# Ten seven-product weight pairs in place of eight, with their weight sums on GpSimd

## The chip, the cores and the metric

The kernel runs on one core of a Trainium2 chip (trn2). The metric is the device time of one execution in microseconds (us). The time before is 927.12 us, the median of 3 runs (926.98 to 927.13).

## What is computed

One decoder layer over 512 tokens with 1024 channels, all in fp32: an RG-LRU branch and a sparse-attention branch, merged by gates, then a feed-forward part (ConvGLU) and a gated per-layer embedding. The change lies in the up projection of the feed-forward part:

```python
xn = _rmsnorm(x, ffn_norm[l])
up = xn @ w_up[l]                     # (512, 1024) @ (1024, 6144)
g_ffn = _causal_dwconv(up[..., :D_FF], ffn_conv_w[l], ffn_conv_b[l])
x = x + (jax.nn.gelu(g_ffn) * up[..., D_FF:]) @ w_down[l]
```

## The kernel before, in words

**Layout.** Channels lie on the 128 partitions and the 512 tokens along the free dimension. Weights are tiles of 128 x 1024 numbers (8 blocks of 128 x 128, one for each 128 input channels). Every fp32 operand of a product is split into a high and a low part in the format fp32r: a cast on ScalarE (ACT) makes the high part, a subtraction on VectorE (DVE) the low one (`split`, L92 to L97; `pair`, L114). One product block is then three matmuls (`three`, L99 to L102): high x high, high x low, low x high. So an output tile of 128 x 512 is 8 x 3 = 24 matmuls of 512 columns on TensorE (PE).

**Order of the work.** The list `order` holds one entry per weight tile or pair of tiles; the main loop (L1013) runs its entries in turn. `feed` (L998) splits weights some entries ahead and issues the next loads on SyncE's (SP) queue. `whi` and `wlo` have four buffers each, `raw` two. What the program text gives is a priority: outside the start (a hand-written schedule), the instructions of each engine are put in order by a scheduler at build time, which lets an instruction go ahead of its place when its inputs and buffers are free in its reckoning. On the chip each engine then takes its instructions in that fixed order.

**The feed-forward part** takes the 24 channel blocks f of the hidden layer in three groups of eight. In each group the up projection comes first: per f the gate half (`up_g`, L586) and the value half (`up_u`, L606), 48 matmuls of 512 columns, which I call an ordinary pair. The gate half passes a three-tap convolution and a GELU (`up_act`, L596), and is multiplied by the value half (L610). In the first group the factor `rstd` of the norm is applied to the products, once on DVE (L591) and once on GpSimd (L603), since it isn't ready earlier; the later groups work on an input that already has it. Then eight down-projection steps (`dn_step`, L613) add the group's part to the residual `F`.

**Seven-product pairs.** For some f of the second and third group (`SEVEN`, L45: 8, 10, ..., 22) gate and value half are done together as a 2 x 2 block product over (first 512 and last 512 input channels) x (gate and value) with half the tokens each, in Strassen's manner: seven products instead of eight, each 4 blocks x 3 matmuls of 256 columns, 84 matmuls in all. They need four weight operands (a, b, c, d), each with a high and a low part, and sums of the input (`xsum`, made by `seven_x`, L168, ahead of the second group). For a pair i:

- `seven_load` (L133) loads both weight tiles into `pairraw` (one buffer, 2 x 512 KB, two transfers on SP's queue).
- `seven_first` (L146) splits the gate tile (operand a, into `whi` and `wlo`) and makes the sums `pairsum` (L153, L154).
- `seven_second` (L156) splits these sums into operand b and makes two more sums in place in `pairraw` (L159, L160).
- `seven_third` (L162) splits the result into c, `seven_last` (L165) splits half of the value tile into d.
- `seven_step` (L189) runs the products, collects them in the PSUM banks p1 to p4 (`aux`, five banks) and drains them on DVE (L218, L220, L224, L229, L233 to L235).

The tiles `bhi`, `blo`, `chi`, `clo`, `dhi`, `dlo`, `pairraw` and `pairsum` have one buffer each. The products stand in the text as a, a, b x sx(0), c x sx(1), c x gx(4), b x sx(2), d; between the last two writes into p3 the text has a read of p3:

```python
prod(p3[:, :h], c, 512, gx(4, second))                            # L223
nc.vector.tensor_add(gp[:, 2 + h:], gp[:, 2 + h:], p3[:, :h])     # L224
...
prod(p3[:, h:], b, 0, sx(2))                                      # L228
```

Of the kernel before, what the change touches and what calls it, by code (L numbers as in the profile page):

```python
# [41 lines left out]

SEG = [0, 128, 384, 768]

SEVEN = tuple(range(8, 24, 2))  # L45
PTO = [0, 512, 1024, 896]


# [1 line left out]
def layer(ctx: ExitStack, tc: tile.TileContext, xT, pT, wall, vwi, vec, relb, onehot, out):  # L50
# [25 lines left out]
    def aux_tile():  # L76
        return psum.tile([128, T], F32, name="aux", bufs=5)
# [53 lines left out]
        return i < len(order) and order[i][0] is None  # L131

    def seven_load(i):  # L133
        f = SW["of"][i]
        SW[i] = r = P["pool"].tile([128, 2, WCOL], F32, name="pairraw")
        for z in range(2):
            nc.sync.dma_start(r[:, z], wall[S_UP + 2 * f + z])

    def seven_pair(i, name, src):
        n = src.shape[1]  # L140
# [5 lines left out]
    def seven_first(i):  # L146
        r = SW[i]
        HI[i] = base.tile([128, WCOL], F32R, name="whi", bufs=NSPL)
        LO[i] = base.tile([128, WCOL], F32R, name="wlo", bufs=NSPL)
        nc.scalar.copy(HI[i], r[:, 0])  # L150
        nc.vector.tensor_sub(LO[i], r[:, 0], HI[i].bitcast(F32))
        s = SW[i, "s"] = P["pool"].tile([128, WCOL], F32, name="pairsum")
        nc.vector.tensor_add(s[:, :512], r[:, 0, :512], r[:, 1, :512])  # L153
        nc.vector.tensor_add(s[:, 512:], r[:, 1, :512], r[:, 1, 512:])  # L154

    def seven_second(i):  # L156
        r, s = SW[i], SW[i, "s"]
        seven_pair(i, "b", s)
        nc.vector.tensor_add(r[:, 0, :512], s[:, 512:], r[:, 0, :512])  # L159
        nc.vector.tensor_add(r[:, 0, 512:], r[:, 0, :512], r[:, 0, 512:])  # L160

    def seven_third(i):  # L162
        seven_pair(i, "c", SW[i][:, 0])

    def seven_last(i):  # L165
        seven_pair(i, "d", SW[i][:, 1, 512:])

    def seven_x(j):  # L168

# [16 lines left out]
        nc.vector.scalar_tensor_tensor(d, b, -1.0, y[1][:, :h], op0=OP.mult, op1=OP.subtract)  # L186
        pair(SW["x"][:, j], t)

    def seven_step(i, f):  # L189
        h = T // 2  # L190
        XG, X = P["XG"], SW["x"]
        first, second = slice(0, h), slice(h, T)

        def prod(o, w, at, x):
            for j in range(4):
                s = slice(at + j * 128, at + (j + 1) * 128)
                xh, xl = x(j)
                three(o, w[0][:, s], w[1][:, s], xh, xl, j == 0, j == 3)

        def gx(k0, t):  # L200
            return lambda j: (XG[:, k0 + j, 0, t], XG[:, k0 + j, 1, t])

        def sx(z):
            t = slice(z * h, (z + 1) * h)
            return lambda j: (X[:, j, 0, t], X[:, j, 1, t])

        seven_third(i)
        a, b, c = (HI[i], LO[i]), SW[i, "b"], SW[i, "c"]
        keep = tmp()
        p1, p2 = aux_tile(), aux_tile()  # L210
        prod(p1[:, :h], a, 0, gx(0, first))
        nc.scalar.copy(keep[:, :h], p1[:, :h])
        seven_last(i)
        prod(p2[:, :h], a, 512, gx(4, first))
        feed(i + 1)
        prod(p2[:, h:], b, 512, sx(0))
        prod(p1[:, h:], c, 0, sx(1))
        nc.vector.tensor_add(keep[:, h:], keep[:, :h], p1[:, h:])  # L218
        gp = P["gp"][f % 2]
        nc.vector.tensor_add(gp[:, 2:], keep, p2)  # L220
        feed(i + 2)
        p3 = aux_tile()
        prod(p3[:, :h], c, 512, gx(4, second))  # L223
        nc.vector.tensor_add(gp[:, 2 + h:], gp[:, 2 + h:], p3[:, :h])  # L224
        if seven(i + 3):
            feed(i + 3)
        g = up_act(f, gp)
        prod(p3[:, h:], b, 0, sx(2))  # L228
        nc.vector.tensor_add(keep[:, h:], keep[:, h:], p3[:, h:])  # L229
        p4 = aux_tile()  # L230
        prod(p4[:, :h], SW[i, "d"], 0, sx(3))
        t = tmp()
        nc.vector.tensor_add(t[:, h:], keep[:, h:], p2[:, h:])  # L233
        nc.vector.tensor_add(t[:, :h], keep[:, h:], p4[:, :h])
        nc.vector.scalar_tensor_tensor(t, t, -1.0, g, op0=OP.mult, op1=OP.mult)  # L235
        defer(pair, hp(f), t)


    urgent, patient, later = [], [], []
# [13 lines left out]
    def defer(f, *a):  # L253
        later.append((f, a))
# [599 lines left out]
    for m in range(8):  # L854
        add(S_OUT + m, lambda i, m=m: out_step(i, m), 0.0,
            open_ffn if m == 0 else (lambda m=m: load_x(m + 1) if m + 1 < 8 else None))
    SW["of"] = {}
    for g in range(3):
        for f in range(8 * g, 8 * g + 8):
            if f in SEVEN:  # L860
                SW["of"][len(order)] = f
                order.append((None, lambda i, f=f: seven_step(i, f), 0.0, None))
                continue
            add(S_UP + 2 * f, lambda i, f=f: up_g(i, f, [(7, stats)] if f == 0 else []))
            add(S_UP + 2 * f + 1, lambda i, f=f: up_u(i, f))
# [129 lines left out]
    n = len(order)  # L995
    at = [9, 11]

    def feed(upto):  # L998
        while at[0] <= min(upto, n - 1):
            i = at[0]  # L1000
            if seven(i):
                seven_first(i)
            else:
                split(i)
            at[0] += 1
            while at[1] < min(at[0] + 2, n):
                if seven(at[1]):
                    seven_load(at[1])
                else:
                    load(at[1])  # L1010
                at[1] += 1

    for i in range(8, n):  # L1013
        if not seven(i):
            feed(i + (1 if seven(i + 1) else 2))
        run_deferred()
        if seven(i + 1):
            seven_second(i + 1)
        _, fn, budget, before = order[i]
        if before:  # L1020
# [68 lines left out]
```

## Time and profile before

| | |
|---|---|
| Median of 3 runs | 927.12 us (926.98 to 927.13) |
| The profiled execution | 926.65 us |
| Its span in the profile | 924.9 us |
| PE busy | 913.7 us (99%), 4486 matmuls |
| DVE busy | 660.7 us (71%) |
| ACT busy | 457.6 us (49%) |
| GpSimd (POOL) busy | 16.1 us (2%) |
| Moved by DMA | 97.24 MB, mean 105 GB/s |

The span is the time from the first to the last recorded instruction. Busy time of PE is modelled, since matmuls overlap: the distance between the starts of neighbouring matmuls tells more of its pace than their durations. PEld is the load of weights into PE, which runs beside the matmuls. A wait is put down to whatever ended last before the waiting instruction started.

### The profile page before, as it was taken

What the parts mean: (1) busy time and instruction counts of PE and PEld (TensorE: products, weight loads), DVE (VectorE), ACT (ScalarE), POOL (GpSimd) and SP (SyncE); (2) the same over time, 40 slices, a digit from 0 to 9 for tenths busy, and PEclk for the clock granted to TensorE, in tenths of its full rate; (3) what the DMA queues carried; (4) which work ended last, traced back from release to release, by engine and by line L of the source; (5) the groups of instructions that cost most, each with busy time, mean ns of one, the idle gap of its engine ahead of it and who ended that gap; (6) DMA issues with size and microseconds to landing.
All of it is one profiled execution on the core that took longest, in us unless ns stands there. A gap on an engine that the chain in (4) does not pass through costs nothing.

```text
span 924.9 us, 11724 instructions
## 1 busy us (share of the span) xinstructions
PE 913.7 (99%) x4486; PEld 770.9 (83%) x4486; DVE 660.7 (71%) x1081; ACT 457.6 (49%) x662; POOL 16.1 (2%) x25
## 2 busy tenths in 40 slices
PE   7999999999999999999999999999999999999998
PEld 6988778888888788888888888888888899988886
DVE  6589798899975877655567557987863587655653
ACT  7477849953223677632444335635542254434530
POOL 0001000000000000000001110000000000000000
PEclk9999999999999999999999999999999999999999
DMA  7463123224233221224532332233322322222231
GB/s 265 121 212 131 46 92 112 70 92 137 92 114 125 80 68 47 69 91 150 176 108 92 98 107 91 69 114 114 114 90 93 115 91 91 91 90 93 91 114 45
DMA packets 31447, 97.24 MB, mean 105 GB/s; under 512 B 3736, under 2 KB 4760, under 8 KB 31392
## 3 DMA queue, kind: packets, MB, share of 16 engines
q1 hardware_dynamic: 31088, 96.38, 31.8%
q8 instruction: 35, 0.57, 0.3%
q10 hardware_dynamic: 304, 0.12, 0.1%
q14 instruction: 20, 0.16, 0.1%
HBM read 92.27 MB, written 4.74 MB: 105 GB/s over the span
## 4 chain that ended last, share of the span: by engine, by line
PE 62%; ACT 2%; DVE 0%; issue 0%; ACTq 0%
PE acc L100 17%; PE acc L101 17%; PE acc L102 17%; PE aux L100 4%; PE aux L101 4%; PE aux L102 4%; ACT E L503 0%; ACT L768 0%; PE aux L516 0%; ACT whi L96 0%; DVE PT L118 0%; ACT L503 0%; ACT gb L768 0%; ACT PT L117 0%; ACT gb L534 0%; DVE tmp L656 0%
## 5 line engine op out<-in xcount | busy, mean ns | idle before, releaser
L96 ACT CAST whi<-raw 128x1024 fp32r<-128x1024 f32 (+1 forms) x140 | 146.1, 1046 | 225.1 <-PE acc L101 165.5
L100 PE MATMUL acc<-XN,whi 128*128 128x512 f32 x632 | 248.8, 394 | 5.0 <-ACT whi L685 5.0
L101 PE MATMUL acc<-XN,whi 128*128 128x512 f32 x632 | 247.9, 392 | 0.0
L102 PE MATMUL acc<-XN,wlo 128*128 128x512 f32 x632 | 247.5, 392 | 0.0
L97 DVE TENSOR_TENSOR wlo<-raw,whi 128x1024 fp32r<-128x1024 f32 (+1 forms) x140 | 169.6, 1214 | 36.7 <-ACT whi L96 36.0
L100 PEld LDWEIGHTS acc<-XN,whi 128*128 128x128 f32 x632 | 119.3, 189 | 28.7 <-ACT whi L685 5.0
L102 PEld LDWEIGHTS acc<-XN,wlo 128*128 128x128 f32 x632 | 119.2, 189 | 24.9
L101 PEld LDWEIGHTS acc<-XN,whi 128*128 128x128 f32 x632 | 119.3, 189 | 24.2 <-DVE XN L121 0.7
L100 PE MATMUL acc<-XG,whi 128*128 128x512 f32 x320 | 124.6, 389 | 0.0
L101 PE MATMUL acc<-XG,whi 128*128 128x512 f32 x320 | 124.6, 389 | 0.0
L102 PE MATMUL acc<-XG,wlo 128*128 128x512 f32 x320 | 124.5, 389 | 0.0
L102 PEld LDWEIGHTS acc<-XG,wlo 128*128 128x128 f32 x320 | 60.1, 188 | 12.6
L100 PEld LDWEIGHTS acc<-XG,whi 128*128 128x128 f32 x320 | 60.1, 188 | 12.2
L101 PEld LDWEIGHTS acc<-XG,whi 128*128 128x128 f32 x320 | 60.1, 188 | 12.1
L616 DVE TENSOR_TENSOR F<-F,acc 128x512 f32<-128x512 f32 x24 | 16.4, 685 | 36.7 <-PE acc L102 36.7
L600 DVE SCALAR_TENSOR_TENSOR tmp<-gp,vc,tmp 128x512 f32<-128x512 f32 x48 | 36.0, 749 | 3.2 <-ACT tmp L598 1.8
L601 ACT ACTIVATE tmp<-tmp 128x512 f32<-128x512 f32 x24 | 15.2, 632 | 31.3 <-DVE tmp L600 31.3
L117 ACT CAST XN<-tmp 128x512 fp32r<-128x512 f32 x32 | 19.9, 621 | 18.9 <-DVE tmp L235 13.0
L354 DVE MAX8 m<-mask 128x8 f32<-128x512 f32 (+2 forms) x48 | 26.6, 558 | 0.7
L610 DVE TENSOR_TENSOR tmp<-tmp,acc 128x512 f32<-128x512 f32 x16 | 11.0, 688 | 22.2 <-POOL tmp L603 14.4
L355 DVE MATCH_REPLACE8 mask<-m,mask 128x512 f32<-128x512 f32 (+2 forms) x48 | 26.1, 544 | 0.0
L100 PE MATMUL acc<-Y,whi 128*128 128x512 f32 x64 | 24.9, 389 | 0.0
(281 smaller groups left out, 1522.6 us busy)
## 6 DMA issues: line engine op xcount, KB each, us to landing
raw<-in_wall SPq DMA_DIRECT2D x137, 512.0 KB, 3.4
pairraw<-in_wall SPq DMA_DIRECT2D x16, 512.0 KB, 4.1
bias_d<-bv_d SPq DMA_DIRECT2D x8, 320.0 KB, 6.2
F<-in_xT SPq DMA_DIRECT2D x8, 256.0 KB, 5.1
QO<-qt SPq DMA_DIRECT2D x16, 128.0 KB, 2.3
bias<-bias_d SPq DMA_DIRECT2D x8, 256.0 KB, 2.7
tmp<-in_xT SPq DMA_DIRECT2D x8, 256.0 KB, 3.7
out_dram<-tmp SPq DMA_DIRECT2D x7, 256.0 KB, 2.3
```

What stands on the lines that cost most here:

```text
L96: nc.scalar.copy(HI[i][:, :n], RAW[i][:, :n])
L97: LAST[0] = nc.vector.tensor_sub(LO[i][:, :n], RAW[i][:, :n], HI[i][:, :n].bitcast(F32))
L100: nc.tensor.matmul(o, lh, rh, start=start, stop=False)
L101: nc.tensor.matmul(o, lh, rl, start=False, stop=False)
L102: nc.tensor.matmul(o, ll, rh, start=False, stop=stop)
L117: nc.scalar.copy(dst[:, 0], src)
L354: nc.vector.max(m8, sc)
L355: nc.vector.match_replace(sc, in_to_replace=m8, in_values=sc, imm_value=SENT)
L600: nc.vector.scalar_tensor_tensor(t, gp[:, j:j + T], col(V_FW + 24 * j + f), t, op0=OP.mult, op1=OP.add)
L601: nc.scalar.activation(t, t, AF.Gelu_apprx_tanh)
L610: nc.vector.tensor_mul(t, GL[f], a)
L616: nc.vector.tensor_add(F[:, m], F[:, m], a)
```

## The change

`SEVEN` becomes a list of ten channel blocks, so that four of them directly follow another one (9 after 8, 12 after 11, 17 after 16, 20 after 19). The four sums of each pair are issued on GpSimd instead of DVE. In `seven_step` the product b x sx(2) moves to the fourth place, ahead of the two products of c, and p3 is allocated together with p1 and p2. What is done with the gate and value halves is passed in as functions (`upper`, `lower`). Loads are issued by a function `loads` of its own, which is also called behind `seven_last`; a flag (`SW["busy"]`) holds the next pair's load, and the loads behind it, back until the present pair's d has been split. The calls of `feed` and `seven_second` get conditions for a pair that directly follows.

```diff
--- before.py
+++ after.py
@@ -42,7 +42,7 @@
 
 SEG = [0, 128, 384, 768]
 
-SEVEN = tuple(range(8, 24, 2))
+SEVEN = (8, 9, 11, 12, 14, 16, 17, 19, 20, 22)
 PTO = [0, 512, 1024, 896]
 
 
@@ -131,10 +131,10 @@
         return i < len(order) and order[i][0] is None
 
     def seven_load(i):
-        f = SW["of"][i]
+        SW["busy"] = True
         SW[i] = r = P["pool"].tile([128, 2, WCOL], F32, name="pairraw")
         for z in range(2):
-            nc.sync.dma_start(r[:, z], wall[S_UP + 2 * f + z])
+            nc.sync.dma_start(r[:, z], wall[SW["of"][i] + z])
 
     def seven_pair(i, name, src):
         n = src.shape[1]
@@ -150,20 +150,21 @@
         nc.scalar.copy(HI[i], r[:, 0])
         nc.vector.tensor_sub(LO[i], r[:, 0], HI[i].bitcast(F32))
         s = SW[i, "s"] = P["pool"].tile([128, WCOL], F32, name="pairsum")
-        nc.vector.tensor_add(s[:, :512], r[:, 0, :512], r[:, 1, :512])
-        nc.vector.tensor_add(s[:, 512:], r[:, 1, :512], r[:, 1, 512:])
+        nc.gpsimd.tensor_add(s[:, :512], r[:, 0, :512], r[:, 1, :512])
+        nc.gpsimd.tensor_add(s[:, 512:], r[:, 1, :512], r[:, 1, 512:])
 
     def seven_second(i):
         r, s = SW[i], SW[i, "s"]
         seven_pair(i, "b", s)
-        nc.vector.tensor_add(r[:, 0, :512], s[:, 512:], r[:, 0, :512])
-        nc.vector.tensor_add(r[:, 0, 512:], r[:, 0, :512], r[:, 0, 512:])
+        nc.gpsimd.tensor_add(r[:, 0, :512], s[:, 512:], r[:, 0, :512])
+        nc.gpsimd.tensor_add(r[:, 0, 512:], r[:, 0, :512], r[:, 0, 512:])
 
     def seven_third(i):
         seven_pair(i, "c", SW[i][:, 0])
 
     def seven_last(i):
         seven_pair(i, "d", SW[i][:, 1, 512:])
+        SW["busy"] = False
 
     def seven_x(j):
 
@@ -186,7 +187,8 @@
         nc.vector.scalar_tensor_tensor(d, b, -1.0, y[1][:, :h], op0=OP.mult, op1=OP.subtract)
         pair(SW["x"][:, j], t)
 
-    def seven_step(i, f):
+    def seven_step(i, dst, upper, lower, banks):
+
         h = T // 2
         XG, X = P["XG"], SW["x"]
         first, second = slice(0, h), slice(h, T)
@@ -207,33 +209,48 @@
         seven_third(i)
         a, b, c = (HI[i], LO[i]), SW[i, "b"], SW[i, "c"]
         keep = tmp()
-        p1, p2 = aux_tile(), aux_tile()
+        p1, p2, p3 = (banks() for z in range(3))
         prod(p1[:, :h], a, 0, gx(0, first))
         nc.scalar.copy(keep[:, :h], p1[:, :h])
         seven_last(i)
+        loads()
         prod(p2[:, :h], a, 512, gx(4, first))
-        feed(i + 1)
+        if not seven(i + 1):
+            feed(i + 1)
         prod(p2[:, h:], b, 512, sx(0))
+        prod(p3[:, h:], b, 0, sx(2))
+        feed(i + (1 if seven(i + 1) or seven(i + 2) else 2))
         prod(p1[:, h:], c, 0, sx(1))
         nc.vector.tensor_add(keep[:, h:], keep[:, :h], p1[:, h:])
-        gp = P["gp"][f % 2]
-        nc.vector.tensor_add(gp[:, 2:], keep, p2)
-        feed(i + 2)
-        p3 = aux_tile()
+        nc.vector.tensor_add(dst, keep, p2)
         prod(p3[:, :h], c, 512, gx(4, second))
-        nc.vector.tensor_add(gp[:, 2 + h:], gp[:, 2 + h:], p3[:, :h])
-        if seven(i + 3):
+        nc.vector.tensor_add(dst[:, h:], dst[:, h:], p3[:, :h])
+        if seven(i + 1):
+            seven_second(i + 1)
+        elif seven(i + 3) and not seven(i + 2):
             feed(i + 3)
-        g = up_act(f, gp)
-        prod(p3[:, h:], b, 0, sx(2))
+        upper()
         nc.vector.tensor_add(keep[:, h:], keep[:, h:], p3[:, h:])
         p4 = aux_tile()
         prod(p4[:, :h], SW[i, "d"], 0, sx(3))
         t = tmp()
         nc.vector.tensor_add(t[:, h:], keep[:, h:], p2[:, h:])
         nc.vector.tensor_add(t[:, :h], keep[:, h:], p4[:, :h])
-        nc.vector.scalar_tensor_tensor(t, t, -1.0, g, op0=OP.mult, op1=OP.mult)
-        defer(pair, hp(f), t)
+        lower(t)
+
+    def seven_up(i, f):
+        gp = P["gp"][f % 2]
+
+        def upper():
+            if f < 8:
+                nc.vector.tensor_mul(gp[:, 2:], gp[:, 2:], rstd)
+            GL[f] = up_act(f, gp)
+
+        def lower(t):
+            nc.vector.scalar_tensor_tensor(t, t, -1.0, GL[f], op0=OP.mult, op1=OP.mult)
+            defer(pair, hp(f), t)
+
+        seven_step(i, gp[:, 2:], upper, lower, aux_tile)
 
 
     urgent, patient, later = [], [], []
@@ -854,12 +871,12 @@
     for m in range(8):
         add(S_OUT + m, lambda i, m=m: out_step(i, m), 0.0,
             open_ffn if m == 0 else (lambda m=m: load_x(m + 1) if m + 1 < 8 else None))
-    SW["of"] = {}
+    SW["of"], SW["busy"] = {}, False
     for g in range(3):
         for f in range(8 * g, 8 * g + 8):
             if f in SEVEN:
-                SW["of"][len(order)] = f
-                order.append((None, lambda i, f=f: seven_step(i, f), 0.0, None))
+                SW["of"][len(order)] = S_UP + 2 * f
+                order.append((None, lambda i, f=f: seven_up(i, f), 0.0, None))
                 continue
             add(S_UP + 2 * f, lambda i, f=f: up_g(i, f, [(7, stats)] if f == 0 else []))
             add(S_UP + 2 * f + 1, lambda i, f=f: up_u(i, f))
@@ -995,6 +1012,16 @@
     n = len(order)
     at = [9, 11]
 
+    def loads():
+        while at[1] < min(at[0] + 2, n):
+            if seven(at[1]):
+                if SW["busy"]:
+                    break
+                seven_load(at[1])
+            else:
+                load(at[1])
+            at[1] += 1
+
     def feed(upto):
         while at[0] <= min(upto, n - 1):
             i = at[0]
@@ -1003,18 +1030,13 @@
             else:
                 split(i)
             at[0] += 1
-            while at[1] < min(at[0] + 2, n):
-                if seven(at[1]):
-                    seven_load(at[1])
-                else:
-                    load(at[1])
-                at[1] += 1
+            loads()
 
     for i in range(8, n):
         if not seven(i):
             feed(i + (1 if seven(i + 1) else 2))
         run_deferred()
-        if seven(i + 1):
+        if seven(i + 1) and not seven(i):
             seven_second(i + 1)
         _, fn, budget, before = order[i]
         if before:
```

## Rows read from the trace of the kernel before

**Rows 1.** Page, sections 1, 2 (40 slices, tenths of full clock) and 4 (chain).

```profile
PE 913.7 (99%) x4486; PEld 770.9 (83%) x4486; DVE 660.7 (71%) x1081; ACT 457.6 (49%) x662; POOL 16.1 (2%) x25
...
PEclk9999999999999999999999999999999999999999
...
PE 62%; ACT 2%; DVE 0%; issue 0%; ACTq 0%
```

**Rows 2.** Waits of PE, the whole span: us in total, times, longest us.

```profile
PE acc L100 <- ACT whi L685: 5.0, 1, 5.0
PE aux L462 <- ACT tmp L456: 1.6, 2, 1.4
```

**Rows 3.** Timeline, POOL and DVE: start us, us, engine, line, operation, [idle before <-releaser].

```profile
510.55 1.29 POOL L603 TENSOR_TENSOR tmp<-tmp,rstd 128x512 f32<-128x512 f32 x1 [8.69 <-ACT tmp L601]
521.43 1.28 POOL L603 TENSOR_TENSOR tmp<-tmp,rstd 128x512 f32<-128x512 f32 x1 [9.59 <-ACT tmp L601]
...
522.74 0.69 DVE L610 TENSOR_TENSOR tmp<-tmp,acc 128x512 f32<-128x512 f32 x1 [2.06 <-POOL tmp L603]
```

**Rows 4.** Chain in order of time: start us, us, what (first matmul of b x sx(2)).

```profile
638.49 0.30 PE aux L100
...
659.64 0.30 PE aux L100
```

**Rows 5.** Timeline, PE, the pair of f=8.

```profile
609.39 0.28 PE L100 MATMUL aux<-XG,whi 128*128 128x256 f32 x1
...
616.58 0.28 PE L100 MATMUL aux<-xsum,dhi 128*128 128x256 f32 x1
...
617.06 0.28 PE L101 MATMUL aux<-xsum,dhi 128*128 128x256 f32 x1
617.26 0.39 PE L100 MATMUL aux<-xsum,bhi 128*128 128x256 f32 x1
...
617.48 0.28 PE L101 MATMUL aux<-xsum,bhi 128*128 128x256 f32 x1
```

**Rows 6.** Timeline, DVE, the same pair.

```profile
616.78 0.42 DVE L224 TENSOR_TENSOR gp<-gp,aux 128x256 f32<-128x256 f32 x1 [0.29 <-PE aux L102]
```

**Rows 7.** Groups by line, 560 to 800 us: busy us, mean ns | idle before.

```profile
L151 DVE TENSOR_TENSOR wlo<-pairraw,whi 128x1024 fp32r<-128x1024 f32 x8 | 9.8, 1224 | 0.9 <-ACT whi L150 0.6
...
L142 ACT CAST chi<-pairraw 128x1024 fp32r<-128x1024 f32 x8 | 8.4, 1049 | 22.8 <-PE aux L101 19.6 <-DVE pairraw L160 3.1
...
L160 DVE TENSOR_TENSOR pairraw<-pairraw 128x512 f32<-128x512 f32 x8 | 5.5, 693 | 0.3
...
L159 DVE TENSOR_TENSOR pairraw<-pairsum,pairraw 128x512 f32<-128x512 f32 x8 | 5.5, 688 | 0.1
L153 DVE TENSOR_TENSOR pairsum<-pairraw 128x512 f32<-128x512 f32 x8 | 5.5, 687 | 4.1 <-DMA pairraw<-in_wall 4.1
L154 DVE TENSOR_TENSOR pairsum<-pairraw 128x512 f32<-128x512 f32 x8 | 5.5, 684 | 0.0
...
L212 ACT COPY tmp<-aux 128x256 f32<-128x256 f32 x7 | 2.6, 373 | 1.3 <-PE aux L102 1.2
```

**Rows 8.** Timeline, ACT and DVE, the pair of f=10.

```profile
637.81 1.05 ACT L142 CAST chi<-pairraw 128x1024 fp32r<-128x1024 f32 x1 [3.27 <-PE aux L101]
...
640.97 0.61 ACT L142 CAST dhi<-pairraw 128x512 fp32r<-128x512 f32 x1
...
644.09 0.69 DVE L143 TENSOR_TENSOR dlo<-pairraw,dhi 128x512 fp32r<-128x512 f32 x1
```

**Rows 9.** Timeline, SP's queue, the next load of a pair.

```profile
644.85 0.80 SPq L137 DMA_DIRECT2D pairraw<-in_wall  x2
```

**Rows 10.** Tile pairraw, all its transfers.

```profile
DMA to landing us min/median/max: 3.1/4.1/6.5
```

**Rows 11.** Windows: us, busy of PE, PEld, DVE, ACT, POOL (x), PEclk, DMA, GB/s.

```profile
651.69:672.84 21.15, 21.15 (x134) 19.14 (x133) 16.98 (x24) 10.64 (x15) 0.00 (x0) 1.00 0.29 100
...
521.43:532.31 10.88, 10.88 (x49) 9.01 (x48) 5.85 (x7) 4.09 (x5) 1.28 (x2) 1.00 0.30 101
```

## The prediction

> **What bounds the kernel now.** I read the page first. TensorE (PE) is busy 99% of the span, at the granted clock's upper level (2.4 GHz) throughout, and the chain that ended last is PE work from end to end, 2% ACT beside it [rows 1]. Next come PE's own waits: two in the whole trace, 5.0 us at the start and 1.6 us in the attention [rows 2], none in the feed-forward part that the change touches. So a change here is worth what it takes from PE's time, as long as nothing else comes late.
>
> Then the length of one pair of weight tiles (gate and value of one f), in the two ways in which the kernel does it. An ordinary pair is 48 matmuls of 512 columns; the one GpSimd multiply that each ordinary pair of the first group makes recurs every 10.88 us (510.55, 521.43) [rows 3]. One seven-product pair and one ordinary pair take 21.15 us together (638.49 to 659.64; the same distance three times there and twice in the last group) [rows 4]. So a seven-product pair takes 21.15 - 10.88 = 10.27 us, only 0.61 us less than an ordinary one.
>
> Where do its 10.27 us go? The pair of f=8 starts at 609.39, and its 65th matmul at 617.06: 64 steps in 7.67 us, 0.1198 us each [rows 5]. 84 of them would be 10.07 us. The other 0.20 us sit in one place: the next matmul starts at 617.26 and the one behind it at 617.48, 0.42 us for two steps that should be 0.24. That matmul is the first of the product b x sx(2), which writes the second half of bank p3. VectorE (DVE) reads the first half of p3 at L224 from 616.78 for 0.42 us, to 617.20 [rows 6]: PE waits for that read. It happens in every such pair, since in the order of before the read of p3 stands between its two halves.
>
> **The change, part by part.**
>
> *Two more seven-product pairs.* Eight become ten: 2 x (10.88 - 10.07) = 1.62 us less on PE, with the 0.20 us wait gone; 2 x 0.61 = 1.22 us with it.
>
> *The products' order.* b x sx(2) moves up to the fourth place, ahead of both c products; p3 is allocated with p1 and p2. Both halves of p3 are now written before DVE reads either, so the wait has no cause left. p1's second half follows the ScalarE (ACT) copy of its first half by three products (4.3 us), and p4 has its own bank; five aux banks for four per step let each bank of a second direct pair be read out, by the drains behind the first pair's last product, before it is written again. I see no new wait of this kind. Bounds: 0.20 us lost per pair as now, or none; a new wait of the same size would be no worse. I take none: the wait fits one instruction, and that instruction now comes later. That is 8 x 0.20 = 1.60 us for the old eight pairs; for the new two it is already counted.
>
> *The sums on GpSimd.* Four additions of 128x512 per pair leave DVE: 0.69 us each, 2.75 us per pair, 22 us over eight pairs [rows 7]. DVE doesn't bound PE, so this is worth nothing by itself. GpSimd takes 1.29 us for such an operation [rows 3]: 5.2 us per pair, 51 us over ten, on an engine that is busy 2% [rows 1]. The latency per two sums grows from 1.4 to 2.6 us, which the lead below hides. In that row DVE idled 2.06 us until GpSimd was done, so no trace of before shows both at work on SBUF operands. Bounds: GpSimd 1.29 us and DVE undisturbed, or each operation first waits for a DVE subtraction of 1.22 us [rows 7] and then holds DVE up for its own 1.29 us. For the sum I take the row as it is, since PE waits for neither; the other end goes into the rivals.
>
> The Trainium skill, "SBUF — State Buffer", section "Who interferes with whom", says that a VectorE instruction with two SBUF inputs and a GpSimd instruction that reads SBUF exclude each other, the later one waiting until the other is through. No row here shows that or its absence. By that rule this part speaks against the change: DVE would lose more time than it is relieved of, and at its worst the sum would come to the second rival's 929.5 us in place of 923.9.
>
> *Pairs in direct sequence* (8-9, 11-12, 16-17, 19-20). Each of the tiles for b, c, d and the raw pair exists once. Let the first pair's step start at 0. b's tiles come free after four products, at 5.75; a cast of 1.05 and a subtraction of 1.22 later [rows 7] the second pair's b is there at 8.0, and it is wanted at 10.07 + 2.88 = 12.95. c: free at 8.63, there at 10.9, wanted at 15.8. d: free at 10.07, there soon after 11.4, wanted at 18.7. The lead is 4.9 us at least. How such casts are served can be seen: chi starts 3.27 us after ACT's last work, when PE frees its tile, and dhi follows the last d product at once; dlo, queued behind other DVE work, comes 3.1 us after dhi started, 2.5 later than alone [rows 8]. So 2.4 us of the lead is safe, and that is enough.
>
> The raw load: it is issued when the tile's last reader is done; dlo ends at 644.78 and the load goes out at 644.85, 14.3 us after the earlier pair's step started (609.39 + 21.15 = 630.54) [rows 8, 9], and lands in 4.1 us [rows 10]. Around a pair 11 the same readers are through some 4 us after pair 9's end, while PE has 10.88 us of ordinary work there: the load of pair 12 goes out about 7 us before step 11 starts, 17 before it is needed. The flag that holds loads back moves it in program order behind pair 11's d tiles, which it waits for in any case. Behind it on SP's queue stand the two raw loads of the next ordinary pair; they are wanted a whole pair later still. Bytes stay the same.
>
> *Load of the other engines.* DVE is busy 16.98 us in 21.15 with one pair of each kind, 5.85 in 10.88 in an ordinary pair of the first group [rows 11], of which 0.69 is a multiply that the later groups don't have. So an ordinary pair costs it 5.16, a seven-product pair 11.82, without the sums 9.07. Two and one: 23.3 of PE's 31.0 us. ACT, 10.64 of 21.15 [rows 11], gains some 3 us over the two pairs. Both are covered.
>
> **Sum:** 1.62 + 1.60 = 3.2 us off PE. The profiled execution took 926.65 us (span 924.9), 0.47 below the median of the runs; it becomes 923.4, and the median 927.12 - 3.2 = 923.9.
>
> **Rivals.**
>
> *A wait stays in each step* (0.20 us, at p3 or where the new order puts a read between two halves of a bank). For it: PE's order isn't the text's: b x sx(2), which the text has ahead of d, starts in the middle of d's matmuls [rows 5], so an order can come out that I don't foresee. Against it: what PE waited for is known. The gain is then 1.22 us: 925.9.
>
> *DVE becomes the bound*, with each GpSimd operation holding it up, as the upper bound above has it. Eight GpSimd operations in two direct pairs and an ordinary one put 8 x 1.29 = 10.3 us on DVE's 23.3: 33.6 against PE's 31.0, 2.6 behind per such three steps, 5.2 in each of the two groups. Against the 2.4 us of safe lead 2.8 is left over, 5.6 in both groups: 929.5. With the whole 4.9 us it is 0.6, and without any lead 10.4. For it: most DVE work here reads two SBUF tiles. Against it: every single operation has to collide, and DVE has gaps. (The rule of the Trainium skill's "SBUF — State Buffer" named above would bring this case about.)
>
> *The second pair's raw load is late*, the case that ends slower by most. Its place is the first pair's step. If it goes out only where the text has it, after the first product (1.44), the copy (0.37), dhi (0.61) and dlo (0.69) [rows 7, 8], at 3.1, then b is there at 3.1 + 4.1 + 2.6 + 2.3 = 12.1 and c at 14.7: in time still. With every sum kept waiting for a DVE subtraction, c takes four times 2.51 us: 3.1 + 4.1 + 10.0 + 2.3 = 19.5 against 15.8, 3.7 us late. Four direct sequences: 14.8 us, 938.7; one: 927.6. It decides from a load issued later than 0.6 us before the step on, and only with the sums delayed; the rows have loads going out far earlier [rows 9].
>
> **How the numbers follow.** Forecast 0.60; a wait stays 0.23; DVE bound 0.11; late load 0.06. A difference of 0.2%, 1.85 us, is about what a measurement of this kernel can tell from no change. The forecast is faster by 0.35%; the first rival is within the bound; the others are slower. The exclusion in part, within the lead, belongs to the forecast. So faster 0.60, same 0.23, slower 0.17. The range runs from 923.2 (the profiled execution's level, less 3.2 and the rounding of eight periods) through the first rival's 925.9 to 927.6, where one direct sequence stalls.
>
> **What would show it.** Right: two neighbouring seven-product pairs start 10.07 us apart; the step between the b product and its neighbours is 0.12 us everywhere, without a 0.2 us hole; 72 more matmuls on PE; GpSimd busy about 67 us; PE's waits still only the two. In the second pair of a sequence chi and bhi wait for PE, not for GpSimd. A wait that stays shows as a hole of 0.2 us per step, ended by DVE or ACT. Exclusion shows as GpSimd operations over 1.3 us or DVE subtractions over 1.22 us where they overlap, or as gaps ended by nothing the trace names; it costs only if PE then waits for blo or clo. A late load shows as PE waiting in pairs 9, 12, 17, 20, with GpSimd sums that start inside the first pair's step. I am wrong if seven-product pairs take longer than 10.3 us, or if PE waits in these steps at all.

## The result, and the profile after

The changed kernel takes 934.39 us, the median of 6 runs (932.8 to 935.25); the kernel before, run beside it, 927.05 us. The ratio is 1.0075, 95% interval 1.0065 to 1.0084: slower by 7.3 us, where 3.2 us less were forecast. The profiled execution took 934.68 us, its span is 932.9 us.

The page of the changed kernel, sections 1 and 4:

```profile
PE 914.8 (98%) x4558; PEld 775.0 (83%) x4558; DVE 663.7 (71%) x1065; ACT 458.2 (49%) x666; POOL 89.2 (10%) x65
...
PE 50%; DVE 6%; ACT 3%; issue 2%; POOL 2%; DMA 2%; SPq 0%; POOLq 0%; DVEq 0%; ACTq 0%
```

PE has the 72 more matmuls of the two new pairs, but the last chain, 62% PE and 2% ACT before [rows 1], now has 6% DVE, 3% ACT, 2% GpSimd and 2% loads of the raw pair in it. DVE is busy 663.7 us, 3.0 more than before, although the sums, 27.5 us for ten pairs, have left it; and GpSimd is busy 89.2 us, where I had expected 67.

The waits of PE (us in total, times, longest):

```profile
PE acc L100 <- ACT whi L702: 5.0, 1, 5.0
PE aux L100 <- ACT tmp L214: 4.8, 2, 2.4
PE aux L479 <- ACT tmp L473: 1.9, 3, 1.4
PE aux L100 <- DVE tmp L224: 1.6, 2, 0.8
```

To the two waits of before [rows 2] come two in the feed-forward part: for DVE's L224 (the first drain of bank p1) and for ACT's L214 (the copy of p1's first half). Where do they sit? The timeline of PE over the pairs 8 and 9, then 11 and 12:

```profile
609.60 0.28 PE L100 MATMUL aux<-XG,whi 128*128 128x256 f32 x1
...
629.75 0.40 PE L100 MATMUL acc<-XG,whi 128*128 128x512 f32 x1
...
640.66 0.28 PE L100 MATMUL aux<-XG,whi 128*128 128x256 f32 x1
...
652.40 0.28 PE L102 MATMUL aux<-XG,wlo 128*128 128x256 f32 x1
653.47 0.38 PE L100 MATMUL aux<-XG,whi 128*128 128x256 f32 x1 [0.79 <-DVE tmp L224]
...
662.20 0.40 PE L100 MATMUL acc<-XG,whi 128*128 128x512 f32 x1
```

Pairs 8 and 9 take 20.15 us together, 10.07 each as forecast, and the hole of 0.20 us [rows 5] is gone. Pairs 11 and 12 take 21.54 us (640.66 to 662.20): in pair 12 PE stands still between 652.40 and 653.47 (some 0.3 us more go in pair 11, where the first c product starts at 646.66, right behind the copy L214). The last group repeats it: 20.16 us, then 21.40 us.

Pair 14, which follows an ordinary pair, is worse. Its timeline on PE, and the windows of pair 13, of pair 14, and of two stretches of pair 14 (us, busy of PE, PEld, DVE, ACT, POOL, then the granted clock, DMA share, GB/s):

```profile
678.74 0.28 PE L102 MATMUL aux<-xsum,blo 128*128 128x256 f32 x1
681.40 0.58 PE L100 MATMUL aux<-xsum,chi 128*128 128x256 f32 x1 [2.38 <-ACT tmp L214]
681.78 0.41 PE L101 MATMUL aux<-xsum,chi 128*128 128x256 f32 x1
681.99 0.41 PE L102 MATMUL aux<-xsum,clo 128*128 128x256 f32 x1
```

```profile
662.20:673.10 10.90, 10.90 (x50) 9.01 (x49) 7.04 (x9) 6.22 (x8) 6.84 (x4) 1.00 0.18 67
673.10:687.24 14.14, 11.76 (x86) 11.55 (x85) 13.08 (x14) 6.85 (x10) 3.70 (x2) 0.88 0.47 157
681.00:683.00 2.00, 1.60 (x7) 1.60 (x8) 2.00 (x2) 0.87 (x3) 2.00 (x2) 0.56 0.41 145
683.00:685.00 2.00, 2.00 (x13) 2.00 (x12) 1.95 (x2) 0.84 (x2) 1.65 (x1) 0.58 0.62 238
```

PE waits 2.66 us from one start to the next in place of 0.12; in the two windows from 681 to 685 the granted clock is 0.56 and 0.58 in the mean, which is mostly the lower of its two levels (1.2 GHz), and matmuls start 0.21 us apart. Pair 14 takes 14.14 us: 10.07, 2.54 for the stall and 1.5 for the clock behind it. Pair 22 takes 14.19. Against 10.07 us per pair the two groups lose 1.4 + 4.1 and 1.2 + 4.1 = 10.8 us. What the two new pairs and the new order gain in these groups is 3.0 us, by e1 below; 10.8 lost and 3.0 gained is +7.8, beside +8.0 between the spans of the two profiled executions and +7.3 between the medians.

**What held PE up.** The groups of GpSimd (busy us, mean ns | idle before):

```profile
L153 POOL TENSOR_TENSOR pairsum<-pairraw 128x512 f32<-128x512 f32 x10 | 20.8, 2082 | 118.2 <-DMA pairraw<-in_wall 76.3 <-DVE xsum L118 27.0 <-DVE gp L225 14.9
L154 POOL TENSOR_TENSOR pairsum<-pairraw 128x512 f32<-128x512 f32 x10 | 20.2, 2019 | 0.0
L160 POOL TENSOR_TENSOR pairraw<-pairraw 128x512 f32<-128x512 f32 x10 | 17.0, 1699 | 0.8
L159 POOL TENSOR_TENSOR pairraw<-pairsum,pairraw 128x512 f32<-128x512 f32 x10 | 15.5, 1554 | 43.8 <-DVE wlo L151 43.1
L620 POOL TENSOR_TENSOR tmp<-tmp,rstd 128x512 f32<-128x512 f32 x8 | 10.3, 1284 | 119.9 <-ACT tmp L618 119.9
```

An operation of two 128x512 inputs takes 1284 ns at L620, where DVE idles, and 1554 to 2082 ns in the mean at L153 to L160. DVE loses too. Around pair 12, the load on SP's queue, then GpSimd, then DVE:

```profile
639.03 0.81 SPq L137 DMA_DIRECT2D pairraw<-in_wall  x2
...
643.77 2.05 POOL L153 TENSOR_TENSOR pairsum<-pairraw 128x512 f32<-128x512 f32 x1 [8.42 <-DMA pairraw<-in_wall]
645.79 2.27 POOL L154 TENSOR_TENSOR pairsum<-pairraw 128x512 f32<-128x512 f32 x1
648.14 2.15 POOL L159 TENSOR_TENSOR pairraw<-pairsum,pairraw 128x512 f32<-128x512 f32 x1
650.38 1.63 POOL L160 TENSOR_TENSOR pairraw<-pairraw 128x512 f32<-128x512 f32 x1
...
645.18 3.97 DVE L97 TENSOR_TENSOR wlo<-raw,whi 128x1024 fp32r<-128x1024 f32 x2
649.07 1.78 DVE L118 TENSOR_TENSOR XN<-tmp,XN 128x512 fp32r<-128x512 f32 x1
650.77 2.31 DVE L143 TENSOR_TENSOR blo<-pairsum,bhi 128x1024 fp32r<-128x1024 f32 x1
653.01 0.41 DVE L224 TENSOR_TENSOR tmp<-tmp,aux 128x256 f32<-128x256 f32 x1
```

The load of pair 12 went out at 639.03, only 1.6 us before pair 11's step began at 640.66. So its four sums run from 643.77 to 652.01, inside that step, and take 8.2 us. In the same time DVE's two subtractions L97 take 3.97 us (2.4 before), L118 takes 1.78 (0.69), blo 2.31 (1.22): some 3.7 us later than without GpSimd. L224, which drains pair 11's bank p1, stands behind them in DVE's queue. Its input was ready when PE had done the first c product, at about 648.1 (646.66 and one product of 1.44); it ran at 653.01, and PE waits for that bank.

The drains themselves, with one input in PSUM, don't stretch. Earlier, around pair 9's end, on GpSimd and DVE:

```profile
628.19 2.32 POOL L153 TENSOR_TENSOR pairsum<-pairraw 128x512 f32<-128x512 f32 x1 [12.12 <-DMA pairraw<-in_wall]
...
630.05 0.42 DVE L237 TENSOR_TENSOR tmp<-tmp,aux 128x256 f32<-128x256 f32 x1
```

L237 takes its 0.42 us in the midst of GpSimd's L153.

In pair 14 the delay goes through two queues. ACT's, DVE's and again ACT's rows:

```profile
667.72 1.06 ACT L142 CAST bhi<-pairsum 128x1024 fp32r<-128x1024 f32 x1 [3.72 <-POOL pairsum L154]
668.68 0.81 ACT L615 ACTIVATE tmp<-gp,vc 128x512 f32<-128x512 f32 x1
...
669.52 1.45 DVE L617 SCALAR_TENSOR_TENSOR tmp<-gp,vc,tmp 128x512 f32<-128x512 f32 x1 [2.98 <-ACT tmp L615]
...
677.43 1.53 DVE L617 SCALAR_TENSOR_TENSOR tmp<-gp,vc,tmp 128x512 f32<-128x512 f32 x2
...
678.99 0.63 ACT L618 ACTIVATE tmp<-tmp 128x512 f32<-128x512 f32 x1 [2.97 <-DVE tmp L617]
...
680.98 0.36 ACT L214 COPY tmp<-aux 128x256 f32<-128x256 f32 x1
```

ACT's cast bhi of pair 14 waits 3.72 us for GpSimd's sum. Behind it stands L615, the first step of pair 12's convolution; DVE idles 2.98 us until that is done, and then has pair 14's splits and pair 13's convolution on its hands. ACT in turn waits 2.97 us for this, and behind that wait stands L214, the copy for which PE waits. None of these instructions is itself slow to compute; each stands behind one that waits.

### The profile page after: what moved, and what is told of

Same layout as the page of the kernel before. It is cut to its first block, busy times and chain, and to the rows that moved or that the text cites. A ratio compares the mean times of both kernels' runs of the same rounds, so it can differ in the third digit from the quotient of the medians.

```text
span 932.9 us, 11931 instructions
## 1 busy us (share of the span) xinstructions
PE 914.8 (98%) x4558; PEld 775.0 (83%) x4558; DVE 663.7 (71%) x1065; ACT 458.2 (49%) x666; POOL 89.2 (10%) x65
## 4 chain that ended last, share of the span: by engine, by line
PE 50%; DVE 6%; ACT 3%; issue 2%; POOL 2%; DMA 2%; SPq 0%; POOLq 0%; DVEq 0%; ACTq 0%
PE acc L101 14%; PE acc L100 14%; PE acc L102 14%; PE aux L100 3%; PE aux L101 3%; PE aux L102 3%; DMA pairraw<-in_wall 2%; DVE tmp L617 1%; DVE wlo L97 1%; POOL pairsum L154 1%; DVE XN L118 0%; DVE blo L143 0%; ACT E L520 0%; POOL pairraw L160 0%; ACT whi L96 0%
## 5 line engine op out<-in xcount | busy, mean ns | idle before, releaser
L96 ACT CAST whi<-raw 128x1024 fp32r<-128x1024 f32 (+1 forms) x136 | 141.6, 1045 | 203.1 <-PE acc L101 150.2
L97 DVE TENSOR_TENSOR wlo<-raw,whi 128x1024 fp32r<-128x1024 f32 (+1 forms) x136 | 171.4, 1264 | 20.3 <-ACT whi L96 19.7
L100 PE MATMUL acc<-XG,whi 128*128 128x512 f32 x288 | 112.1, 389 | 0.0
L101 PE MATMUL acc<-XG,whi 128*128 128x512 f32 x288 | 112.1, 389 | 0.0
L102 PE MATMUL acc<-XG,wlo 128*128 128x512 f32 x288 | 112.0, 389 | 0.0
L102 PEld LDWEIGHTS acc<-XG,wlo 128*128 128x128 f32 x288 | 54.1, 188 | 11.2
L100 PEld LDWEIGHTS acc<-XG,whi 128*128 128x128 f32 x288 | 54.1, 188 | 11.1
L101 PEld LDWEIGHTS acc<-XG,whi 128*128 128x128 f32 x288 | 54.1, 188 | 11.0
L617 DVE SCALAR_TENSOR_TENSOR tmp<-gp,vc,tmp 128x512 f32<-128x512 f32 x48 | 39.4, 820 | 8.0 <-ACT tmp L615 7.2
L153 POOL TENSOR_TENSOR pairsum<-pairraw 128x512 f32<-128x512 f32 x10 | 20.8, 2082 | 118.2 <-DMA pairraw<-in_wall 76.3
L118 DVE TENSOR_TENSOR XN<-tmp,XN 128x512 fp32r<-128x512 f32 x32 | 25.2, 788 | 4.1 <-ACT XN L117 4.1
```

The source lines that it names most:

```text
L96: nc.scalar.copy(HI[i][:, :n], RAW[i][:, :n])
L97: LAST[0] = nc.vector.tensor_sub(LO[i][:, :n], RAW[i][:, :n], HI[i][:, :n].bitcast(F32))
L100: nc.tensor.matmul(o, lh, rh, start=start, stop=False)
L101: nc.tensor.matmul(o, lh, rl, start=False, stop=False)
L102: nc.tensor.matmul(o, ll, rh, start=False, stop=stop)
L118: nc.vector.tensor_sub(dst[:, 1], src, dst[:, 0].bitcast(F32))
```

## The experiments

Three theories at first. **A:** the one raw tile turns over too slowly with slow sums in its circle. **B:** GpSimd and DVE exclude each other, and DVE becomes the bound. **C:** direct sequence is too tight by itself. Each edit is against the changed kernel unless said otherwise. The medians of the kernel before, beside these runs, lay between 926.73 and 926.81 us.

**Sums back on DVE, ten pairs** (e1).

```diff
-        nc.gpsimd.tensor_add(s[:, :512], r[:, 0, :512], r[:, 1, :512])
-        nc.gpsimd.tensor_add(s[:, 512:], r[:, 1, :512], r[:, 1, 512:])
+        nc.vector.tensor_add(s[:, :512], r[:, 0, :512], r[:, 1, :512])
+        nc.vector.tensor_add(s[:, 512:], r[:, 1, :512], r[:, 1, 512:])
...
-        nc.gpsimd.tensor_add(r[:, 0, :512], s[:, 512:], r[:, 0, :512])
-        nc.gpsimd.tensor_add(r[:, 0, 512:], r[:, 0, :512], r[:, 0, 512:])
+        nc.vector.tensor_add(r[:, 0, :512], s[:, 512:], r[:, 0, :512])
+        nc.vector.tensor_add(r[:, 0, 512:], r[:, 0, :512], r[:, 0, 512:])
```

> The changed kernel with its four sums per pair back on DVE; ten pairs and the new order stay. Theory A (the one raw tile turns over too slowly: load, four sums, c and d, then the next load, 15.5 to 19.8 us a circle with the sums taking 7 to 8 us on GpSimd, against 16.8 us of PE work per pair in the first mixed group): the sums shrink to about 2.8 us, the circle to some 11 to 15, and the kernel takes about 924 us. Theory B (the exclusion between GpSimd and DVE makes DVE the bound): also about 924, with DVE subtractions back at 1.22 us. Theory C (direct sequence itself is too tight, whichever engine makes the sums): it stays at 930 us or more, with PE waiting in the pairs 12 and 14.

Measured: 923.91 us (923.52 to 924.22), ratio 0.9965 (0.9952 to 0.9978). C falls: direct sequence costs nothing, with the same order of instructions on PE. The new order of products and the two further pairs bring 2.9 us beside the kernel before (926.81), 3.0 in the two groups of the traces, where the forecast had 3.2. The order on ACT and DVE, though, isn't that of the changed kernel: with the sums on another engine the scheduler put these two queues together differently. In e1 the drain L224 of pair 11 stands ahead of the split blo of pair 12, in the changed kernel behind it:

```profile
648.42 0.42 DVE L224 TENSOR_TENSOR tmp<-tmp,aux 128x256 f32<-128x256 f32 x1
648.76 1.22 DVE L143 TENSOR_TENSOR blo<-pairsum,bhi 128x1024 fp32r<-128x1024 f32 x1
```

ACT likewise has pair 14's bhi ahead of pair 12's L615 in the changed kernel, and behind it in e1. So e1 alone doesn't separate what GpSimd holds up from what the other order of the queues does.

One thing speaks against A as I had put it: the load of pair 12 goes out at 640.46 here, later than in the changed kernel, and does no harm. The page, section 1:

```profile
PE 910.8 (99%) x4558; PEld 772.4 (84%) x4558; DVE 669.9 (73%) x1105; ACT 458.7 (50%) x666; POOL 16.1 (2%) x25
```

DVE is busy 669.9 us with the sums (40 x 0.69 = 27.5 us), 642.4 without them. In the changed kernel it was 663.7: GpSimd's 40 operations cost DVE 21.3 us of waiting, and took 73.5 us themselves instead of 51.4. Moving 27.5 us of work off DVE relieved it by 6.2.

**Eight pairs, sums on GpSimd** (e2) **and eight pairs, sums on DVE** (e3).

```diff
-SEVEN = (8, 9, 11, 12, 14, 16, 17, 19, 20, 22)
+SEVEN = tuple(range(8, 24, 2))
```

(e3 has e1's edit as well)

> The changed kernel with the eight pairs of before (8, 10, ..., 22): sums on GpSimd and the new order of products stay. Theory A: one pair per 21 us of PE work, longer than the circle, so no wait of PE: 927.05 - 8 x 0.20 = 925.4 us. Theory B: DVE has some 14.2 us of its own plus at most 5.2 held up per 21 us, so it fits as well: 925.4, but the GpSimd operations still stretch to about 2 us. Theory C: 925.4. If GpSimd alone costs time, apart from direct sequences: above 927.

> The eight pairs of before, sums on DVE: of the change only the new order of the products is left. All theories: the hole of 0.20 us per pair is gone, 8 x 0.20 = 1.6 us less than before, 925.4 us. If the new order is worth nothing, 927.0.

Measured: 925.51 us, ratio 0.9986 (0.9976 to 0.9995), and 925.50 us, ratio 0.9983 (0.9974 to 0.9992). With one pair per 21 us, the engine of the sums makes no difference; the new order of products alone is worth 1.3 us (926.81 to 925.50), a little less than its 1.6: in the trace a pair goes from 10.24 to 10.07 us, so the hole was 0.17 us and not 0.20. The pair of f=8 on PE with DVE's sums, its first matmul and the first of the ordinary pair behind it, 10.07 us later, where it was 10.24 before:

```profile
609.33 0.28 PE L100 MATMUL aux<-XG,whi 128*128 128x256 f32 x1
...
619.40 0.40 PE L100 MATMUL acc<-XG,whi 128*128 128x512 f32 x1
```

**Two raw tiles, ten pairs, sums on GpSimd** (e4).

```diff
-        SW[i] = r = P["pool"].tile([128, 2, WCOL], F32, name="pairraw")
+        SW[i] = r = P["pool"].tile([128, 2, WCOL], F32, name="pairraw", bufs=2)
...
-        P["gp"] = [P["pool"].tile([128, 576], F32, name="gp%d" % z)[:, :T + 2] for z in range(2)]
+        P["gp"] = [P["pool"].tile([128, 520], F32, name="gp%d" % z)[:, :T + 2] for z in range(2)]
```

> The changed kernel with two raw tiles per pair in place of one (room made by cutting the unused ends of the two gp tiles, 576 to 520 wide). Sums stay on GpSimd, ten pairs. Theory A: the load no longer waits for the pair ahead, the circle is broken up, PE no longer waits: 924 to 926 us, although GpSimd and DVE still stretch each other's operations. Theory B: DVE is as loaded as in the changed kernel, so it stays near 934. Theory C: the slots of b, c and d are as before, so it stays near 934.

Measured: 923.78 us, ratio 0.9964 (0.995 to 0.9978). The exclusion is still there; it only falls elsewhere. GpSimd and DVE ahead of pair 11's step, which starts at 640.75 here:

```profile
630.85 2.09 POOL L153 TENSOR_TENSOR pairsum<-pairraw 128x512 f32<-128x512 f32 x1 [6.17 <-DMA pairraw<-in_wall]
...
636.95 1.61 POOL L160 TENSOR_TENSOR pairraw<-pairraw 128x512 f32<-128x512 f32 x1
...
635.65 1.78 DVE L617 SCALAR_TENSOR_TENSOR tmp<-gp,vc,tmp 128x512 f32<-128x512 f32 x1
```

Pair 12's sums now run from 630.85 to 638.56, beside the ordinary pair 10 and ahead of pair 11's step; they are nearly as slow as before (7.7 us against 8.2), and DVE's L617 takes 1.78 us instead of 0.75. But DVE has room there, and PE's waits are those of e1 but for one of 0.3 us. Not all is gone: the pairs 8 and 9 take 19.95 us together, but 11 and 12 take 20.15 and 19 and 20 take 20.47. B in its plain form, DVE too loaded over the whole stretch, falls.

**The narrow gp tiles alone** (e12), as a control.

```diff
-        P["gp"] = [P["pool"].tile([128, 576], F32, name="gp%d" % z)[:, :T + 2] for z in range(2)]
+        P["gp"] = [P["pool"].tile([128, 520], F32, name="gp%d" % z)[:, :T + 2] for z in range(2)]
```

> The changed kernel with nothing but the gp tiles cut from 576 to 520, as in the kernels with two raw tiles. It should stay at the changed kernel's 933 to 935 us: then the second raw tile is what brought those to 923.8. If it falls below 930, the tiles' place in memory has a part in it.

Measured: 932.61 us (two runs, 930.81 and 934.41). So it is the second raw tile that counts for the stalls: PE stands still in the same four places here, for 1.16, 2.81, 1.17 and 2.78 us. Two other things show. The pairs 8 and 9 take 19.94 us, 9.97 each. And in the profiled execution (930.81) the clock stays up behind the two long stalls. The windows of the pairs 14 and 22, in the same columns as above:

```profile
672.28:685.05 12.77, 10.24 (x86) 10.04 (x84) 11.79 (x12) 6.97 (x10) 3.72 (x2) 1.00 0.49 166
802.63:815.37 12.74, 10.24 (x86) 10.04 (x84) 11.59 (x17) 6.37 (x10) 0.00 (x0) 1.00 0.32 100
```

At 1.00 the long stalls cost 2.7 us each and nothing behind them. So the 1.5 us at the lower level are not a fixed part of such a stall. The executions of the changed kernel, from 932.8 to 935.25 us, have mean granted clocks of 0.998 to 0.995.

What remained: is it GpSimd's latency in the chains (**L**) or its hold on DVE (**X**)?

**Half of the sums on GpSimd**: the last two (e5), the first two (e6).

```diff
-        nc.gpsimd.tensor_add(s[:, :512], r[:, 0, :512], r[:, 1, :512])
-        nc.gpsimd.tensor_add(s[:, 512:], r[:, 1, :512], r[:, 1, 512:])
+        nc.vector.tensor_add(s[:, :512], r[:, 0, :512], r[:, 1, :512])
+        nc.vector.tensor_add(s[:, 512:], r[:, 1, :512], r[:, 1, 512:])
```

(e5; e6 does the same with the other two, L159 and L160)

> Ten pairs, one raw tile; the first two sums (b) on DVE, the last two (toward c) on GpSimd. Theory L (what costs is that ACT and DVE, which take their work in order, stand still until GpSimd's slow sums are there, above all the cast of b, 21.8 us of waiting in the changed kernel): b no longer waits for GpSimd, so PE's stalls go: 924 to 926 us. Theory X (what costs is DVE being held up by GpSimd's reads of SBUF, whoever waits for them): half of the operations are left, so about half of the 10.5 us that the sums on GpSimd cost: 928 to 930.

> Ten pairs, one raw tile; the first two sums (b) on GpSimd, the last two on DVE. Theory L: the cast of b still waits some 4 us for GpSimd behind the load, with other work behind it on ACT; only the wait of c goes: 927 to 932 us, worse than with the last two sums on GpSimd. Theory X: as with the last two, 928 to 930.

Measured: 928.0 us (926.71 to 928.99), ratio 1.0011 (1.0002 to 1.0021), and 926.68 us, ratio 0.9999 (0.999 to 1.0008). Each half costs, 4.1 and 2.8 us above e1, and both together 10.5. That e5 is the slower of the two is against L; e6 lies below what X gave. These two alone don't decide.

**GpSimd at work with nobody waiting for it**: four additions per pair that read the finished sums (e9), four fills instead (e10). Both start from e1 and write `rstd`, which nothing reads in this stretch.

```diff
+        if SW["of"][i] > S_UP + 16:
+            for z in range(4):
+                nc.gpsimd.tensor_add(rstd, s[:, :512], s[:, 512:])
```

(e10: `nc.gpsimd.memset(rstd, 0.0)`)

> Ten pairs, all real sums on DVE, and four additions of 128x512 per pair on GpSimd that read the finished sums of b and write a tile nobody reads in this stretch (for nine of the ten pairs). GpSimd's reads of SBUF are there, its latency is not in any chain. Theory X: DVE operations of two SBUF inputs stretch to 1.8 to 2.3 us where they overlap, DVE falls behind, and the time comes out near the changed kernel's: 930 us or more. Theory L: the stretched operations are in the trace as well, but the time stays within 1 us of 923.9.

> As the kernel with four idle additions per pair, but with four fills of 128x512 on GpSimd in their place, which write SBUF and read nothing. If it is GpSimd's reads that exclude DVE's two-input operations, DVE's subtractions stay at 1.22 us and the fills at one duration; if any GpSimd access to SBUF does, both stretch where they overlap. Time in either case near 923.9 us.

Measured: 942.09 us (941.86 to 942.97), ratio 1.0168 (1.0152 to 1.0183), and 923.57 us (one run). From 585 us to the end of the up projection PE, ACT and DVE run the same instructions in the same order in e1, e9 and e10; only GpSimd's work differs. Groups from 605 to 830 us, e9 with the additions first, then e1 without:

```profile
L157 POOL TENSOR_TENSOR rstd<-pairsum 128x512 f32<-128x512 f32 x36 | 64.5, 1791 | 184.4 <-DVE pairsum L154 182.3
...
L143 DVE TENSOR_TENSOR blo<-pairsum,bhi 128x1024 fp32r<-128x1024 f32 x9 | 17.7, 1966 | 3.5 <-ACT bhi L142 3.5
```

```profile
L143 DVE TENSOR_TENSOR blo<-pairsum,bhi 128x1024 fp32r<-128x1024 f32 x9 | 11.0, 1223 | 7.9 <-ACT bhi L142 7.9
```

With the additions blo takes 1966 ns in the mean, without them 1223. The fills of e10 wait for nothing in the pairs and ran elsewhere: all 36 in one go from 591.43 to 612.41, around the start of the first pair, and none beside the later pairs. The group over the whole span, and its end on the timeline (cut off at 600):

```profile
L157 POOL MEMSET rstd<- 128x512 f32 x36 | 19.0, 527 | 27.3 <-DVE tmp L180 25.3
```

```profile
599.62 12.79 POOL L157 MEMSET rstd<- 128x512 f32 x22
```

So e10's time says nothing of fills beside the pairs. But in those 21 us DVE is busy for 18.2 and GpSimd for 19.0, and neither stretches: the pair's sums take 0.68 to 0.69 us, blo at 598.02 takes 1.22, every fill 0.53. PE's waits with the additions (us in total, times, longest), none of which e1 has:

```profile
PE aux L100 <- DVE tmp L236: 4.3, 2, 2.2
PE acc L100 <- ACT XN L117: 3.6, 1, 3.6
PE aux L102 <- DVE clo L143: 2.8, 2, 1.9
```

That is X: 18 us lost (942.09 against e1's 923.91) through additions for whose results nothing in the trace waits, with the order of the queues unchanged. It costs more than the changed kernel's real sums, presumably because here DVE has its own sums to do besides; no run shows the reason.

**Two raw tiles and sums on DVE** (e7): the edits of e1 and e4 together.

> Ten pairs, two raw tiles, all sums on DVE. PE no longer waited with either remedy alone (sums on DVE 923.9 us, two raw tiles 923.8), so both together give the same, 923.8 us, unless DVE (11.8 us per pair against PE's 10.07 in a direct sequence) falls behind in the two direct pairs: then 924 to 926.

Measured: 922.84 us (922.49 to 923.43), ratio 0.9956 (0.9944 to 0.9969). About 1 us better than either edit alone. Its direct pairs take 9.97 us instead of 10.07, which is ten times 0.1 us. That goes with the narrow gp tiles: the undisturbed pairs take 9.97 or 9.98 us in the kernels that have them (e4, e7, e11, e12), with one raw tile or two and with the sums on either engine, and 10.07 in those that don't (e1, e2, e3, e10). Why, no run shows. So the second raw tile by itself takes nothing off e1's time, and e4 had the same 1 us but for the 0.7 that its pairs 11 and 12, 19 and 20 lost.

**Twelve pairs, two raw tiles**: sums on GpSimd (e8, on top of e4) and on DVE (e11, on top of e7).

```diff
-SEVEN = (8, 9, 11, 12, 14, 16, 17, 19, 20, 22)
+SEVEN = (8, 9, 10, 12, 13, 14, 16, 17, 18, 20, 21, 22)
```

> Twelve pairs, three in direct sequence each time (8-9-10, 12-13-14 and the same in the last group), two raw tiles, sums on GpSimd. If the raw tile was all that stood in the way: two more pairs at 10.07 in place of 10.88 us, 923.8 - 1.6 = 922.2 us. If three in sequence use up the lead (the tiles b, c, d exist once, DVE 9.1 us of its own per pair plus up to 5.2 held up against PE's 10.07): PE waits in the third pair of a sequence, 925 us or more.

> Twelve pairs, three in direct sequence each time, two raw tiles, all sums on DVE. If GpSimd's reads were what slowed the twelve pairs with sums on GpSimd (929.4 us), this takes 922.8 - 2 x 0.81 = 921.2 us. If three in sequence are too many for DVE by itself (11.8 us per pair against PE's 10.07) or for the single tiles of b, c and d, PE waits in the third pair and the time is above 923.

Measured: 929.39 us, ratio 1.0025 (1.0013 to 1.0036), and 920.91 us, ratio 0.9941 (0.9924 to 0.9958). Three pairs in sequence are not too many for the tiles or for DVE, even with its sums; with GpSimd's hold on DVE they are. PE's waits with GpSimd's sums are for the same two sorts of instruction as in the changed kernel, ACT's copy of p1 (L214, 3.7 us) and a drain on DVE (L233, 0.8 us); with DVE's sums PE waits nowhere in this part.

The twelve pairs with sums on DVE are the fastest kernel of this study, 5.8 us below the kernel before and 13.5 below the changed one.

## Why the prediction was wrong

*The two new pairs and the order of products* came out nearly as worked out: 10.07 us per pair, no hole, 3.0 us off the two groups in e1 against 3.2. The hole was taken 0.03 us per pair too large (0.42 us for two steps of 0.24 leaves 0.18, and the pair of f=8 took 10.24 us, not 10.27).

*The sums on GpSimd* is the step that failed. It took the row of before "as it is, since PE waits for neither" [rows 3], and that row had DVE idle. With both at work the additions took 1.55 to 2.08 us in the mean, and DVE lost 21 us (less than the 27.5 it was relieved of, so the prediction's reading of the rule went too far there). The rule of the Trainium skill, "SBUF — State Buffer", section "Who interferes with whom", which I gave no weight in the sum, agrees with the runs: operations of DVE with two inputs in SBUF stretch beside additions (1.22 to 2.31 us, 0.69 to 1.78), drains that have one input in PSUM don't (L237, 0.42 us), and fills, which read nothing, hold up nobody (e10, 591 to 612 us). In the rows shown an operation of either side was held up by at most 1.1 us, a little less than a whole addition of 1.28.

*Pairs in direct sequence* counted the wrong lead. I reckoned when the weights b, c and d would be there, found 4.9 us, and they were indeed in time. PE waited for drains instead: L224 and L214 stand in the queues of DVE and ACT behind the next pair's splits, and have no such lead. I had also put the load of pair 12 at 7 us before pair 11's step; it went out 1.6 us before, since its last readers, clo and dlo of pair 11, came late. By itself that does no harm (e1, 640.46). With sums on GpSimd it moves 8 us of hold-up into the one stretch where drains are due.

*The rivals.* DVE held up by GpSimd was there as the second rival, with 0.11 and 929.5 us. The mechanism was right; the price was worked out from the sum of DVE's work, as if only its whole surplus counted, and it lacked the queues and the granted clock: each of the two long stalls cost 2.5 us, and in the profiled execution 1.5 more at the lower clock level, which e12 shows to come and go. The third rival had the place right, sums that begin inside the first pair's step, but named c as what would be late, and it wasn't.

*What stays open:* how much of pair 14's stall is bhi's wait for GpSimd's result, and how much DVE's lateness from before. e9 shows that the hold-up alone is enough to stall PE, not that it is all there is in the changed kernel. The other order of ACT's and DVE's queues is a rival that no run takes apart from it. In pair 12 it looks as if both were needed: 3.7 us earlier L224 would have run at 649.3, and ahead of blo, as in e1, at about 650.8, each well before PE wanted the bank at 652.5. I didn't try to move the drains ahead of the splits in the queues with the sums on GpSimd.

## What to carry to other kernels

Before work goes from DVE to an idle GpSimd, look whether DVE will be running operations with two SBUF inputs at that time: here 27 us moved relieved DVE by 6, and the moved work took 43% longer than alone. Where something is hidden by a lead, count the lead of everything that stands in the same queue behind it, the drains that release PE's banks above all, not only of the operand that it makes. And a buffer too few can put the hold-up in the worst place: with ten pairs a second raw tile made the same GpSimd work nearly free (with twelve it still cost 8.5 us), and keeping the sums on DVE made it unnecessary.

## What the runs showed of the hardware

Additions of 128x512 on GpSimd took 1.28 us with DVE idle and up to 2.32 us beside its operations with two inputs in SBUF, which in turn grew by up to 1.1 us; fills of the same size took 0.53 us and stretched nothing in the 21 us in which both engines were at work. After PE had stood still for 2.66 us its granted clock was 0.56 and 0.58 in the two windows that follow (681 to 685 us); after the pause of 1.07 us in pair 12 it stayed at 1.00, and in e12 it stayed at 1.00 after 2.81 and 2.78 us too.
